# Block kernel, prologue: both low-rank projections tile by tile on the raw input, squares behind them and summed in fours, zero stores moved to after the first group

## Chip, cores, metric

One core of one Trainium2 chip. The time is device time in microseconds of one launch of the whole kernel, median of the runs shown. Everything is float32 in memory; products run on TensorE as three passes over split operands (below).

## The reference, cut to what matters

One layer (`DEPTH` 1) over 512 frames of width 1024. The part that the change touches is the first norm and two narrow column blocks of the input projection, 256 of its 11520 columns: `xw` and `xa` (64 columns each, together "lr0") and `xg` (128 columns, "lr1").

```python
h = rms_norm(x, norm1_g[l])
p = h @ w_in[l]
pa, pb, pg, pc = _split(p, (COLS_A, COLS_B, COLS_GATE, COLS_C))
...
pc = token_shift(pc, rwkv_mu[l])
r, k, v, xw, xa, xg = _split(pc, (D_C, D_C, D_C, R_W, R_A, R_G))
w_log = -jax.nn.softplus(-(rwkv_w0[l] + jnp.tanh(xw) @ rwkv_w2[l])) - 0.5
a = jax.nn.sigmoid(rwkv_a0[l] + xa @ rwkv_a2[l])
g_c = jax.nn.sigmoid(xg) @ rwkv_g2[l]
...
yc = rwkv7_recurrence(rh, decay, kh, vh, kk, ah)
...
m = gate_a * y_a + gate_b * y_b + gate_c * y_c
x = x + m @ w_out[l]
h2 = rms_norm(x, norm2_g[l])
x = x + jnp.square(jax.nn.relu(h2 @ mlp_w1[l])) @ mlp_w2[l]
return rms_norm(x, final_g)
```

The norm's factor is one number per frame, so it can be applied behind a projection of the raw, gain-weighted input instead of in front of it. The kernel does so for four projections: lr0, lr1, and the first blocks of k and r.

## The kernel before, in words

Channels lie on the 128 partitions and frames along the row: `xT` is eight tiles of 128 x 512. A projection of one block of 128 columns is a sum over the eight tiles. Each operand is split into a high part, rounded by a cast on ScalarE, and a low part, the difference formed on VectorE; `mm3` (lines 168 to 171) issues three products per tile, high x high, high x low, low x high, so a projection is 24 matmuls of 128 x 512 into one PSUM buffer.

A framework orders the work. Each instruction has a priority by its place in the program; blocks under `high_priority` are moved ahead by their offset; each engine then works through a fixed list, in order. PSUM pools give three projection buffers (`pp`), two of `pm`, and single ones. Weights come through two raw buffers and three high and low ones (`load_w`, `split_w`).

The prologue (lines 229 to 380):

- POOL clears `zer` and fills `ones`. SP loads the lr0 weight in two halves and `xT` in five pieces, the lr1 weight last. `load_half` (line 151) issues a load and the split of it. ScalarE's own queue loads only the norm's gain `n1t`.
- Two products of `ones` with `zer` (line 258) run before there is data. `warm` loads the Tanh table on ScalarE.
- The loop over the eight tiles forms `xgh` and `xgl`, the split of x times gain, then, at raised priority, the square of the tile on ScalarE; after every second tile VectorE adds the two squares and TensorE sums them over channels with `ones` into `pst` (line 274, four plain float32 products, two passes each). Then the three products of lr0 follow.
- `rsqrt_rows` turns `pst` into `rsb`, the reciprocal root for each frame, in some fifteen short VectorE steps.
- lr1 is projected afterwards as one block (`proj_raw`, line 293), then k0 and r0. `unscaled` multiplies a result with `rsb` into `us`, which empties its PSUM buffer. `pro_scale` makes the normalised rows `hh`, `hl`, tile by tile, which all other projections read.

The main part interleaves two sequences of generators. `krv(g)` makes k, r and v of a group of four heads, `amat(g)` the within-chunk matrices, `inverse` their triangular inverses in two rounds, `chain` runs over the eight chunks. The other sequence, "fill" `fl`, is `ab(q)` for eight blocks, eight projections each, later the gates `gate(q)`. `weave(crit, fill, r)` places r steps of fill behind each step of the critical one; R0 is r beside krv(0). A step of either ends at a `yield`.

The four zero stores (line 874) write a block of zeros from `zer` to `ttd` in device memory, which the chain reads after the inverses have filled the rest. They stand behind krv(0) in the program but wait for nothing except the clearing of `zer`.

At the end, each quarter of the output takes a Sqrt on ScalarE (line 1229). Line 1056 applies a Sqrt to the small tile `epst`, line 1057 fills that tile again.

Of the kernel before, what the change touches and what calls it, by code (L numbers as in the profile page):

```python
# [9 lines left out]
F32 = mybir.dt.float32  # L10
# [19 lines left out]
R0, R1, R2, R3 = 0.85, 0.8, 0.85, 1.6  # L30
NWARM = 2
# [68 lines left out]
def block_kernel(ctx, tc, xt, win, par, mulr, sw, wout, w1, w2, fg, cst, eyes, out):  # L100
# [3 lines left out]
    def tt(o, a, b, op):  # L104
        return v.tensor_tensor(out=o, in0=a, in1=b, op=op)  # L105
# [45 lines left out]
    def load_half(w, src, i):  # L151
        sl = slice(i * S, (i + 1) * S)
        sy.dma_start(w[0][:, sl], src[:, sl])
        split_w(w, sl)
# [88 lines left out]
    wlr = [new_w()]  # L243
    load_half(wlr[0], win[CN[("lr", 0)]], 0)
    for a, n in ((0, 1), (1, 1), (2, 2)):
        sy.dma_start(xT[:, a:a + n], xt[a:a + n].rearrange("k p t -> p k t"))
    load_half(wlr[0], win[CN[("lr", 0)]], 1)
    for a, n in ((4, 2), (6, 2)):
        sy.dma_start(xT[:, a:a + n], xt[a:a + n].rearrange("k p t -> p k t"))
    wlr.append(new_w())  # L250
    for i in range(2):
        load_half(wlr[1], win[CN[("lr", 1)]], i)
# [4 lines left out]
    for i in range(NWARM):  # L257
        pe.matmul(wu, ones, zer, start=True, stop=True)
# [4 lines left out]
    t_lr0 = pp.tile([P, S], F32, tag="pp", name="pp")  # L263
    sqp_ctx = ExitStack()
    sqp = sqp_ctx.enter_context(tc.tile_pool(name="sqp", bufs=1))
    for kt in range(KT):
        sq = (p1 if kt % 2 else sqp).tile([P, S], F32, tag=f"v{kt // 2 % 2}" if kt % 2 else f"sq{kt // 2}", name="sq")
        ac.activation(xgh(kt), xT[:, kt], AF.Copy, scale=n1t[:, kt:kt + 1])
        stt(xgl[:, kt], xT[:, kt], n1t[:, kt:kt + 1], f(xgh(kt)), MUL, SUB)
        with tc.high_priority(offset=OFFP):  # L270
            ac.activation(sq, xT[:, kt], AF.Square)
            if kt % 2 == 1:
                tt(sq, sq, sq_, ADD)
                pe.matmul(pst, ones, sq, start=kt == 1, stop=kt == KT - 1)
        mm3(t_lr0, *wslice(wlr[0], kt), xgh(kt), xgl[:, kt], start=kt == 0, stop=kt == KT - 1)
        sq_ = sq
# [67 lines left out]
    t_lr1 = pp.tile([P, S], F32, tag="pp", name="pp")  # L344
    proj_raw(wlr[1], t_lr1)
# [526 lines left out]

    for g in range(NG):
        gp.dma_start(ttd[32:64, g, :, 0:32], zer[0:32, 0:32].unsqueeze(1).to_broadcast([32, NC * 4, 32]))
# [108 lines left out]
    with tc.tile_pool(name="mw", bufs=2) as mw, \  # L983
# [72 lines left out]
        ac.activation(epst, epst, AF.Sqrt)  # L1056
        gp.memset(epst, EPS)
# [258 lines left out]
```

## Time and profile before

| what | us |
|---|---|
| runs of the kernel | 1028.8 median of 3 (1027.36 to 1030.81) |
| the profiled execution, its own time | 1029.49 |
| its span, first to last instruction | 1027.7 |
| TensorE busy | 1007.2 |
| VectorE busy | 735.1 |
| ScalarE busy | 512.9 |

A line of the profile's timeline gives start, duration, engine, program line, operation, written tile, read tiles and shape; in brackets the idle time of the engine before it and what ended it. PE is TensorE, PEld its weight load, DVE is VectorE, ACT is ScalarE, SPq and POOLq are queues that issue transfers. In a table of stages each engine has its busy time in the stage and its instructions; the last three columns are the granted TensorE clock, the busy share of the DMA engines and GB/s. Matmuls overlap at their ends, so durations of 0.39 us follow each other every 0.23 us.

### The profile page before, as it was taken

Reading aid. Unit: us, or ns where it says so; the run is one execution under the profiler, and the core shown is the slowest. Engines: PE = TensorE matmul, PEld = TensorE weight load, DVE = VectorE, ACT = ScalarE, POOL = GpSimd, SP = SyncE. Lnnn points to the kernel's source line nnn. Section 1 sums busy time; section 2 is a strip of 40 time slices with the busy share of each in tenths; the row PEclk is TensorE's granted clock in tenths of the full one; section 3 lists DMA queues with packets and bytes.
Section 4 is the critical chain, followed back from the end, with each engine's and each line's share of the span. In section 5 each row is a group of like instructions: output and inputs, shape, how many; then the busy total and the mean of one; then the engine's idle time right before and its main releaser. Section 6 shows DMA issues by size and latency. Waiting matters only on the chain. (4 is left out here: it accounts for less than half of the span.)

```text
span 1027.7 us, 15699 instructions
## 1 busy us (share of the span) xinstructions
PE 1007.2 (98%) x6110; PEld 817.7 (80%) x6110; DVE 735.1 (72%) x1251; ACT 512.9 (50%) x757; POOL 110.1 (11%) x179
## 2 busy tenths in 40 slices
PE   8999999999999999999999999999999999999997
PEld 5777877888887788888787877888888888878885
DVE  6997497599865886794668779656554546887775
ACT  7756453655554655456446344435433334454344
POOL 1013011201212112001322100100000000000001
PEclk9999999999999999999999999999999999999999
DMA  6444643734546446434897724544333325644442
GB/s 231 129 123 112 185 134 114 215 107 128 150 134 164 136 126 161 158 95 122 268 256 243 220 87 119 174 132 130 90 99 103 98 87 164 226 127 139 143 166 102
DMA packets 49177, 151.53 MB, mean 147 GB/s; under 512 B 6544, under 2 KB 10128, under 8 KB 48080
## 3 DMA queue, kind: packets, MB, share of 16 engines
q1 hardware_dynamic: 34816, 99.93, 30.6%
q0 software_dynamic: 13568, 49.56, 18.0%
q8 instruction: 48, 0.79, 0.3%
q10 hardware_dynamic: 720, 1.05, 0.3%
q14 instruction: 25, 0.20, 0.1%
HBM read 123.78 MB, written 26.74 MB: 146 GB/s over the span
## 5 line engine op out<-in xcount | busy, mean ns | idle before, releaser
L148 ACT CAST whi<-raw 128x1024 fp32r<-128x1024 f32 (+1 forms) x164 | 169.7, 1037 | 257.0 <-PE pp L170 86.7
L105 DVE TENSOR_TENSOR wlo<-raw,whi 128x1024 fp32r<-128x1024 f32 (+1 forms) x176 | 206.5, 1175 | 91.2 <-ACT whi L148 90.6
L169 PE MATMUL pp<-hh,whi 128*128 128x512 f32 x688 | 271.2, 395 | 0.4 <-DVE rs L108 0.4
L170 PE MATMUL pp<-hl,whi 128*128 128x512 f32 x688 | 270.1, 393 | 0.0
L171 PE MATMUL pp<-hh,wlo 128*128 128x512 f32 x688 | 269.1, 391 | 0.2 <-DVE wlo L105 0.2
L169 PEld LDWEIGHTS pp<-hh,whi 128*128 128x128 f32 x688 | 129.1, 188 | 28.9 <-DVE rs L108 0.9
L171 PEld LDWEIGHTS pp<-hh,wlo 128*128 128x128 f32 x688 | 129.2, 188 | 27.5 <-DVE wlo L105 0.6
L170 PEld LDWEIGHTS pp<-hl,whi 128*128 128x128 f32 x688 | 129.2, 188 | 26.3
L169 PE MATMUL p<-h2h,whi 128*128 128x512 f32 x256 | 100.4, 392 | 0.0
L171 PE MATMUL p<-h2h,wlo 128*128 128x512 f32 x256 | 99.7, 389 | 0.0
L170 PE MATMUL p<-h2l,whi 128*128 128x512 f32 x256 | 99.6, 389 | 0.0
L108 DVE SCALAR_TENSOR_TENSOR r<-p,rsb 128x512 f32<-128x512 f32 x32 | 22.0, 691 | 69.3 <-PE p L171 68.8
L171 PEld LDWEIGHTS p<-h2h,wlo 128*128 128x128 f32 x256 | 48.1, 188 | 10.2
L169 PEld LDWEIGHTS p<-h2h,whi 128*128 128x128 f32 x256 | 48.1, 188 | 9.8
L170 PEld LDWEIGHTS p<-h2l,whi 128*128 128x128 f32 x256 | 48.1, 188 | 9.6
L1225 POOL TENSOR_TENSOR x0f<-xr,fgt 128x512 f32<-128x512 f32 x4 | 5.2, 1296 | 310.6 <-DMA raw<-in_w 301.4
L170 PE MATMUL acc<-ml,whi 128*128 128x512 f32 x64 | 25.0, 391 | 0.0
L171 PE MATMUL acc<-mh,wlo 128*128 128x512 f32 x64 | 25.0, 390 | 0.0
L1076 PE MATMUL acc<-whi,a2h 128*128 128x512 f32 x64 | 24.9, 389 | 0.0
L1076 PE MATMUL acc<-whi,a2l 128*128 128x512 f32 x64 | 24.9, 389 | 0.0
L1076 PE MATMUL acc<-wlo,a2h 128*128 128x512 f32 x64 | 24.9, 389 | 0.0
L1076 PE MATMUL acc<-whi,ah 128*128 128x512 f32 x64 | 24.9, 389 | 0.0
(368 smaller groups left out, 1733.5 us busy)
## 6 DMA issues: line engine op xcount, KB each, us to landing
raw<-in_win SPq DMA_DIRECT2D x88, 512.0 KB, 3.6
raw<-in_w SPq DMA_DIRECT2D x64, 512.0 KB, 3.6
ax<-axd POOLq DMA_DIRECT2D x8, 1024.0 KB, 10.0
axd<-AXt POOLq DMA_DIRECT2D x12, 512.0 KB, 8.7
raw<-in_w SPq DMA_DIRECT2D x24, 256.0 KB, 2.9
bkd<-BKT POOLq DMA_DIRECT2D x4, 1024.0 KB, 15.4
raw<-in_wout SPq DMA_DIRECT2D x8, 512.0 KB, 3.6
bk<-bkd POOLq DMA_DIRECT2D x7, 512.0 KB, 13.0
```

Source lines behind the costliest of these rows:

```text
L105: return v.tensor_tensor(out=o, in0=a, in1=b, op=op)
L108: return v.scalar_tensor_tensor(out=o, in0=a, scalar=s, in1=b, op0=op0, op1=op1)
L148: ac.copy(hi[:, sl], raw[:, sl])
L169: pe.matmul(ps, wh, xh, start=start, stop=False)
L170: pe.matmul(ps, wh, xl, start=False, stop=False)
L171: pe.matmul(ps, wl, xh, start=False, stop=stop)
L1076: pe.matmul(b[i], x_[:, ms], w_, start=id(b[i]) not in begun, stop=last and n == 2, skip_group_check=True)
L1225: gp.tensor_tensor(out=o0, in0=x0, in1=fgt[0], op=MUL)
```

## The change

- Both lr weights are loaded ahead, in halves: the first half of lr1 from ScalarE's queue, the others from SP, between the pieces of x. Their splits stand in the loop, at tiles 0 and 4.
- In the loop each tile has its `xgh` and `xgl`, then the six products of lr0 and lr1, then its square. Squares are added in pairs and the pairs in fours; `pst` has two products instead of four. The raised priority of squares and `pst` goes. lr1 takes a second `pp` buffer from the start; its block behind the loop goes.
- The products before the data are twelve of 128 columns instead of two of 512.
- R0 goes from 0.85 to 1.3.
- The zero stores read a new tile `zz`, from the `vt` buffers, cleared by POOL behind krv(0).
- Lines 1056 and 1057 go.

```diff
-R0, R1, R2, R3 = 0.85, 0.8, 0.85, 1.6
-NWARM = 2
+R0, R1, R2, R3 = 1.3, 0.8, 0.85, 1.6
+NWARM = 12
...
-    wlr = [new_w()]
-    load_half(wlr[0], win[CN[("lr", 0)]], 0)
-    for a, n in ((0, 1), (1, 1), (2, 2)):
+    wlr = [new_w(), new_w()]
+    lr_src = [win[CN[("lr", i)]] for i in range(2)]
+
+    def load_lr(eng, i, h):
+        sl = slice(h * S, (h + 1) * S)
+        eng.dma_start(wlr[i][0][:, sl], lr_src[i][:, sl])
+
+    def load_x(a, n):
         sy.dma_start(xT[:, a:a + n], xt[a:a + n].rearrange("k p t -> p k t"))
-    load_half(wlr[0], win[CN[("lr", 0)]], 1)
-    for a, n in ((4, 2), (6, 2)):
-        sy.dma_start(xT[:, a:a + n], xt[a:a + n].rearrange("k p t -> p k t"))
-    wlr.append(new_w())
-    for i in range(2):
-        load_half(wlr[1], win[CN[("lr", 1)]], i)
+
+    load_lr(sy, 0, 0)
+    load_lr(ac, 1, 0)
+    load_x(0, 1)
+    load_x(1, 1)
+    load_x(2, 2)
+    load_lr(sy, 0, 1)
+    load_lr(sy, 1, 1)
+    load_x(4, 2)
+    load_x(6, 2)
...
     for i in range(NWARM):
-        pe.matmul(wu, ones, zer, start=True, stop=True)
+        pe.matmul(wu[:, 0:P], ones, zer[:, 0:P], start=True, stop=True)
...
-    t_lr0 = pp.tile([P, S], F32, tag="pp", name="pp")
+    t_lr = [pp.tile([P, S], F32, tag="pp", name="pp") for _ in range(2)]
+    t_lr0, t_lr1 = t_lr
...
     for kt in range(KT):
-        sq = (p1 if kt % 2 else sqp).tile(...)
+        if kt % 4 == 0:
+            for w in wlr:
+                split_w(w, slice(kt // 4 * S, kt // 4 * S + S))
         ac.activation(xgh(kt), xT[:, kt], AF.Copy, scale=n1t[:, kt:kt + 1])
         stt(xgl[:, kt], xT[:, kt], n1t[:, kt:kt + 1], f(xgh(kt)), MUL, SUB)
-        with tc.high_priority(offset=OFFP):
-            ac.activation(sq, xT[:, kt], AF.Square)
-            if kt % 2 == 1:
-                tt(sq, sq, sq_, ADD)
-                pe.matmul(pst, ones, sq, start=kt == 1, stop=kt == KT - 1)
-        mm3(t_lr0, *wslice(wlr[0], kt), xgh(kt), xgl[:, kt], start=kt == 0, stop=kt == KT - 1)
+        for w, t in zip(wlr, t_lr):
+            mm3(t, *wslice(w, kt), xgh(kt), xgl[:, kt], start=kt == 0, stop=kt == KT - 1)
+        sq = (p1 if kt % 2 else sqp).tile(...)
+        ac.activation(sq, xT[:, kt], AF.Square)
+        if kt % 2 == 1:
+            tt(sq, sq, sq_, ADD)
+        if kt % 4 == 3:
+            tt(sq, sq, sq4, ADD)
+            pe.matmul(pst, ones, sq, start=kt == 3, stop=kt == KT - 1)
+        if kt % 4 == 1:
+            sq4 = sq
         sq_ = sq
...
-    t_lr1 = pp.tile([P, S], F32, tag="pp", name="pp")
-    proj_raw(wlr[1], t_lr1)
...
     weave(krv(0, GS[0]), fl, R0)
+    zz = p1.tile([P, 2, 2, P], F32, tag="vt", name="zz", bufs=2)[0:32, 0, 0, 0:32]
+    gp.memset(zz, 0.0)
     for g in range(NG):
-        gp.dma_start(ttd[32:64, g, :, 0:32], zer[0:32, 0:32].unsqueeze(1).to_broadcast(...))
+        gp.dma_start(ttd[32:64, g, :, 0:32], zz.unsqueeze(1).to_broadcast(...))
...
-        ac.activation(epst, epst, AF.Sqrt)
-        gp.memset(epst, EPS)
```

More of the change, by code (lines that the diff above doesn't have):

```diff
@@ L266, in block_kernel @@
     for kt in range(KT):
-        sq = (p1 if kt % 2 else sqp).tile([P, S], F32, tag=f"v{kt // 2 % 2}" if kt % 2 else f"sq{kt // 2}", name="sq")
+        if kt % 4 == 0:
+            for w in wlr:
+                split_w(w, slice(kt // 4 * S, kt // 4 * S + S))
         ac.activation(xgh(kt), xT[:, kt], AF.Copy, scale=n1t[:, kt:kt + 1])
         stt(xgl[:, kt], xT[:, kt], n1t[:, kt:kt + 1], f(xgh(kt)), MUL, SUB)
-        with tc.high_priority(offset=OFFP):
-            ac.activation(sq, xT[:, kt], AF.Square)
-            if kt % 2 == 1:
-                tt(sq, sq, sq_, ADD)
-                pe.matmul(pst, ones, sq, start=kt == 1, stop=kt == KT - 1)
-        mm3(t_lr0, *wslice(wlr[0], kt), xgh(kt), xgl[:, kt], start=kt == 0, stop=kt == KT - 1)
+        for w, t in zip(wlr, t_lr):
+            mm3(t, *wslice(w, kt), xgh(kt), xgl[:, kt], start=kt == 0, stop=kt == KT - 1)
+        sq = (p1 if kt % 2 else sqp).tile([P, S], F32, tag=f"v{kt // 2 % 2}" if kt % 2 else f"sq{kt // 2}", name="sq")
+        ac.activation(sq, xT[:, kt], AF.Square)
[6 more added lines that the diff above has]
+            sq4 = sq
         sq_ = sq
@@ L871, in block_kernel @@
     weave(krv(0, GS[0]), fl, R0)
+    zz = p1.tile([P, 2, 2, P], F32, tag="vt", name="zz", bufs=2)[0:32, 0, 0, 0:32]
+    gp.memset(zz, 0.0)
     for g in range(NG):
-        gp.dma_start(ttd[32:64, g, :, 0:32], zer[0:32, 0:32].unsqueeze(1).to_broadcast([32, NC * 4, 32]))
+        gp.dma_start(ttd[32:64, g, :, 0:32], zz.unsqueeze(1).to_broadcast([32, NC * 4, 32]))
     for g in range(NG):
```

## The prediction

> **What bounds the kernel now.** I read the page first, for the shares of the engines, and then a table of stages, because an average over a millisecond says nothing about the stage that is edited.
>
> ```profile
> span 1027.7 us, 15699 instructions
> ...
> PE 1007.2 (98%) x6110; PEld 817.7 (80%) x6110; DVE 735.1 (72%) x1251; ACT 512.9 (50%) x757; POOL 110.1 (11%) x179
> ```
>
> ```profile
> core 0: us, PE busy (x) PEld busy (x) DVE busy (x) ACT busy (x) POOL busy (x), PEclk, DMA share, GB/s
> 0.00:8.26 8.26, 4.18 (x6) 1.47 (x6) 1.43 (x3) 5.57 (x10) 3.93 (x13) 0.98 0.74 230
> 8.26:16.30 8.04, 7.91 (x22) 4.24 (x21) 6.29 (x10) 7.55 (x13) 0.93 (x3) 0.81 1.02 351
> 16.30:40.00 23.70, 23.70 (x103) 18.89 (x102) 23.41 (x52) 15.36 (x24) 0.58 (x1) 1.00 0.45 144
> ...
> 43.70:80.00 36.30, 35.74 (x154) 28.16 (x154) 35.32 (x87) 24.31 (x37) 3.31 (x5) 1.00 0.36 102
> 80.00:100.00 20.00, 18.60 (x134) 14.46 (x133) 15.87 (x24) 11.41 (x19) 5.57 (x10) 1.00 0.44 131
> ...
> 602.00:640.00 38.00, 38.00 (x197) 30.35 (x194) 33.87 (x63) 17.93 (x29) 2.15 (x4) 1.00 0.36 104
> ...
> 1000.00:1028.00 28.00, 20.42 (x91) 16.56 (x89) 14.85 (x25) 13.27 (x29) 5.18 (x4) 0.95 0.30 111
> ```
>
> TensorE is the bound nearly everywhere: outside the first stage its busy time is the stage itself, to a few per cent. So only what moves TensorE's own order is worth anything, and the place where it is not full is the start. The second thing to see is the DVE column from 16.3 to 80 us: 23.41 of 23.70, then 35.32 of 36.30. Over that stretch VectorE is as full as TensorE. A lead that TensorE gains at the start is therefore not automatically kept.
>
> The start in order of time, where the argument lies:
>
> ```profile
> 0.75 0.39 SPq L153 DMA_DIRECT2D raw<-in_win  x1
> ...
> 1.46 3.49 PE L258 MATMUL wu<-zer,ones 128*128 128x512 f32 x4 [1.46 <-POOL one L255]
> ...
> 2.88 1.28 ACT L1056 ACT_TABLE_LOAD   x1
> ...
> 4.29 0.61 ACT L271 ACTIVATE sq<-xT 128x512 f32<-128x512 f32 x1
> ...
> 6.70 0.60 ACT L148 CAST whi<-raw 128x512 fp32r<-128x512 f32 x1
> 6.83 0.69 DVE L105 TENSOR_TENSOR sq<-sq 128x512 f32<-128x512 f32 x1 [6.83 <-ACT sq L271]
> ...
> 7.21 0.72 ACT L268 ACTIVATE xgh<-xT,n1t 128x512 fp32r<-128x512 f32 x1
> ...
> 7.57 1.75 PE L274 MATMUL pst<-sq,ones 128*128 128x512 f32 x2 [2.62 <-DVE sq L105]
> ...
> 8.33 1.42 PE L169 MATMUL pp<-xgh,whi 128*128 128x512 f32 x1
> ...
> 13.17 1.02 PE L274 MATMUL pst<-sq,ones 128*128 128x512 f32 x2
> 13.62 0.80 PE L170 MATMUL pp<-xgl,whi 128*128 128x512 f32 x1
> ...
> 15.80 0.72 DVE L195 STREAM_TRANSPOSE rqw<-pst 128x512 f32<-128x512 f32 x1
> ```
>
> The first product that counts runs at 8.33. ScalarE squares x first (4.29), and TensorE sits idle from 4.95 until the square sum reaches it. The clock view shows what the idle costs:
>
> ```profile
> 10.00:11.00 1.00, 0.88 (x3) 0.28 (x2) 1.00 (x3) 0.67 (x2) 0.00 (x0) 0.50 1.05 404
> ...
> 12.00:13.00 1.00, 0.99 (x4) 0.36 (x3) 0.81 (x2) 1.00 (x3) 0.00 (x0) 1.00 0.99 350
> ```
>
> The granted clock (third column from the end) is 0.50 around 10.5 and 1.00 after 12. The mean of 0.81 over the 8.04 us from 8.26 is 0.19 x 8.04 = 1.5 us of lost clock.
>
> Then TensorE's stream with its marks, the first matmul of the k projection, of the r projection, of the first projection on normalised rows, and where that one runs dry:
>
> ```profile
> 24.39 0.39 PE L169 MATMUL pp<-xgh,whi 128*128 128x512 f32 x1
> ...
> 29.94 0.39 PE L169 MATMUL r<-xgh,whi 128*128 128x512 f32 x1
> ...
> 35.49 0.39 PE L169 MATMUL pp<-hh,whi 128*128 128x512 f32 x1
> ...
> 39.14 0.39 PE L171 MATMUL pp<-hh,wlo 128*128 128x512 f32 x1
> ...
> 40.09 0.66 PE L169 MATMUL pp<-hh,whi 128*128 128x512 f32 x2
> ```
>
> One projection of 24 matmuls is 35.49 - 29.94 = 5.55 us, 0.231 each. And VectorE, which makes the normalised rows:
>
> ```profile
> 23.02 0.71 DVE L202 STREAM_TRANSPOSE rsb<-rqq 128x512 f32<-128x512 f32 x1
> 23.66 1.18 DVE L105 TENSOR_TENSOR wlo<-raw,whi 128x1024 fp32r<-128x1024 f32 x1
> ...
> 27.75 0.74 DVE L108 SCALAR_TENSOR_TENSOR hl<-xT,n1t,hh 128x512 fp32r<-128x512 f32 x1
> ...
> 39.50 0.69 DVE L105 TENSOR_TENSOR us<-pp,rsb 128x512 f32<-128x512 f32 x1
> ...
> 42.97 0.74 DVE L108 SCALAR_TENSOR_TENSOR hl<-xT,n1t,hh 128x512 fp32r<-128x512 f32 x1
> ```
>
> TensorE meets VectorE here with almost no slack: the tiles of `hl` come from 27.75 to 43.6, and the second PSUM buffer of `pp` is free only when `us` at 39.50 has emptied the lr1 result; TensorE starts its second normalised projection at 40.09.
>
> **The change part by part.** *The squares.* Summing in fours takes two of the four `pst` matmuls away. One is two passes; from 13.17 the next matmul, which needs 0.39 by itself, ends at 14.42 and so began its own work near 14.03: 0.86 us each, 1.7 us of TensorE saved. VectorE gets two additions more, at the 0.69 of the 6.83 row, 0.60 where they follow each other: +1.2 us.
>
> *The order.* The splits of both lr weights, `xgh`, `xgl` and the six products of a tile come before its square. The first tile needs the first weight half, the first x tile, two splits and `xgh`. In the trace the first half is issued at 0.75 and ScalarE can read x0 at 4.29. The second half-weight now goes out beside it on ScalarE's queue, 256 KB, which at the 371 to 404 GB/s of the busy rows is 0.7 us more in front of or between the bytes of x0. Two casts at 0.53 pace and one scaled copy at 0.71 from about 4.2 to 4.5 put the first product at 5.8 to 6.2; I take 6.0, 2.3 us earlier than 8.33. From there a tile is six products, 1.39 us on TensorE, against about 1.2 to 1.3 on ScalarE (`xgh` 0.71, square 0.61, both overlapping a little) and 1.1 on VectorE, so TensorE sets the pace except at the second weight halves, two casts of 0.6, for which I allow 0.7 in all. Sum: 6.0 + 48 x 0.231 + 1.7 + 0.7 = 19.5 for both projections, against 24.39: **4.9 us of lead**.
>
> *The bytes.* The zero stores go out between 1.88 and 9.5 on POOL's queue, beside x:
>
> ```profile
> 4.00:5.00 1.00, 0.95 (x2) 0.00 (x0) 0.00 (x0) 0.89 (x3) 0.47 (x1) 1.00 0.78 154
> ...
> 6.00:7.00 1.00, 0.00 (x0) 0.00 (x0) 0.17 (x1) 0.83 (x2) 0.00 (x0) 1.00 1.04 387
> ```
>
> ```profile
> xT<-in_xt SPq DMA_DIRECT2D x1, 512.0 KB, 8.7
> ...
> L874 POOL DMA_DIRECT2D ttd<-zer x4: 784/795/981, 1.9 to 8.7; - x4
> ```
>
> In their slice the engines move 154 GB/s where they move 387 two slices later. Two such slices lose about 0.4 MB, 1.1 us; that pays for most of the 512 KB of lr1, 1.4 us, which now stands ahead of x4 to x7. So the last x tiles land about when they do now (issued near 3.6, 8.7 us to land: 12.3), between 10.8 and 12.6. They are wanted at 13, so this is hidden; were they 2 us later still, TensorE would wait that long.
>
> The Trainium skill, "DMA: Bandwidth & Descriptors", rules for kernel authors, says that issuing from several engines gives no bandwidth, since all run on the same 16 DMA engines. By that rule ScalarE's queue brings nothing sooner and 1.4 us of lr1 bytes count in full; no row here has two hardware queues loading at once, so nothing here confirms it.
>
> *The warm-up.* 12 products of 128 columns instead of 2 of 512: at the 3.49 us for 1024 columns of the 1.46 row, 1536 columns are 5.2 us at the low clock, until 6.7; if the clock rises at about 4.6 the last ones run twice as fast and end near 5.6. Between 0 and 0.7 us in front of the first product; I take 0. What it buys is that TensorE no longer idles before the work: up to the 1.5 us of lost clock, already in the 4.9, whose sum is at full clock.
>
> The Trainium skill, "TensorE: Matmul & The Clock Gate", Part 1, puts the rise behind one busy window of about 3.4 us that runs free of the kernel, and the fall behind an idle one. The trace agrees: busy 3.49 us, idle 2.62, then 0.50 for about three slices. By that rule the phase of the window alone could move the gain by up to 1.5 us between runs.
>
> *The removed square root* on `epst`. It was placed at 2.88, not at the end; its table load of 1.28 is on ScalarE before x has landed, worth nothing there. The reload that it forces later also goes:
>
> ```profile
> 23.35 1.28 ACT L391 ACT_TABLE_LOAD   x1
> ```
>
> That one stands before a weight cast and the shift of lr: 0.3 us at most on the path. The four zero stores reappear after krv(0), at 0.8 us of POOL each and behind the release of a `vt` buffer. The row behind them:
>
> ```profile
> 98.12 1.60 POOL L539 DMA_DIRECT2D lad<-AXt  x2 [11.15 <-DVE AXt L105]
> ```
>
> POOL sits idle for 11.15 us before it, waiting for VectorE; 3.3 us of issue fit in. Uncovered, they would delay those stores by 3.3 us, which only the inverse behind later groups reads. Cost 0.
>
> *The weave, R0 0.85 to 1.3.* krv(0) has 20 steps: 17 fill steps become 26. A fill chain of 8 projections has 32 steps, so a step is 8 x 5.55 / 32 = 1.4 us and 9 steps move 12.5 us of TensorE's work from later to here. It changes no total. It helps where VectorE is full, because fill asks less of VectorE per microsecond; it costs later cover, and the row of 602 to 640 is full, with gates behind the chain of chunks, 35 us of it, against 12.5 taken. I take 0, between -1.4 (the idle of 80 to 100) and +2.
>
> *What comes late next.* TensorE, 4.9 us ahead, reaches the normalised rows at 30.6. VectorE has by the stage table 1.43 + 6.29 + 23.41 + 3.6 = 34.7 us of work up to the last `hl`, in 36.8 us from its first instruction at 6.83. It now starts near 4.2, with 1.2 more to do: 2.6 - 1.2 = 1.4 us of lead if it idles as much as now, 3.5 if it never idles, none if the square sum, now last, holds it up. I take 2.0. The second `pp` buffer then comes free at 38.1 instead of 40.1, with one tile (0.69) more of the first projection behind TensorE: 2.7 us of lead there, and 0.3 from the table load and the gap at 39.14, 3.0; half of the 0.56 us that 43.7 to 80 has of idle is put to the extra fill, 0.2 to 0.3. So TensorE gives 1.7 of its 4.9 back and **3.2 us remain**. The tail is not touched.
>
> The profiled execution took 1029.49, its span and 1.8 us around it, 0.07% above the median 1028.8. Its span should become 1027.7 - 3.2 = 1024.5; the median 1028.8 - 3.2 = **1025.6**.
>
> **The rivals.** *VectorE takes nearly all back.* It is at 99% from 16.3 to 40; if its lead is below 1, TensorE waits for `hl` and the buffer, and only about 1 us is left: 1027.8. For it: the DVE column. Against: weight splits that now sit behind 23.02 can be done before.
>
> *The whole lead is kept.* With the splits of 1.18 out of the way and more fill beside krv(0), TensorE never waits: 4.9 and a little of the idle later, 5.3: 1023.5. For it: 40 to 100 has 2 us of idle to recover. Against: one free `pp` buffer until `us`.
>
> *Slower: the root is late.* The last square sum is now behind all six products of the last tile, near 18.9 instead of 15.8. If the small steps of the root are threaded between long additions as now (15.80 to 23.73, 7.9 us), `rsb` comes at 26.9 instead of 23.73, 3.2 later, and every `hh` and `hl` with it. With the 1.2 of extra additions, less the 0.69 and 0.3 above, the loss is 3.4: 1032.2. It decides, beyond what can be told from no change, from an `rsb` at about 26.6 on. Against: the `xgl` and lr splits that VectorE threads in there now are done earlier.
>
> **How the numbers follow.** The measurement tells about 0.3% from no change, 3.1 us, so 1025.7 and 1031.9 are the limits. The first case, part of the lead kept, has 0.40 and its own range 1024.2 to 1027.0; as it lies on the limit, half of it counts on either side. Nearly all taken back 0.24, all kept 0.24, root late 0.12. Faster 0.20 + 0.24 = 0.44, same 0.20 + 0.24 = 0.44, slower 0.12. TensorE's idle time between start and tail, 1027.7 - 1007.2 less 4.1 before 8.26 and 7.6 in the last 28 us, is 8.8 us; a shifted order deals these waits anew, for which I allow 1.7 us below the whole lead and 2.4 above the case that loses it: 1021.8 to 1030.2.
>
> **What would show it.** First product of `pp` at about 6 and granted clock 1.00 from there; four `pst` passes, not eight; the lr products done at 19 to 20; no table load before Exp; `rsb` at 23 to 26; the first matmul on `hh` near 30, and gaps of some 2 us on TensorE between 30 and 40, put down to `hl` or `us`. Wrong would be: a first product later than 7.5, `rsb` after 27, new gaps in 80 to 110 or in the chain of chunks around 500 to 600.

## The result, and the profile after

The change makes the kernel slower: median 1036.84 us (1035.27 to 1038.19, 6 runs) against 1029.62 us (1027.36 to 1030.81, 6 runs) on the same chip, ratio 1.0071, 95% interval 1.0055 to 1.0088. That is 7.2 us more. The forecast was 1025.6 us with a range up to 1030.2; the time lies outside, on the other side. (Every ratio here is against runs of the kernel before on the same chip.) The profiled execution took 1038.19 us, its span is 1036.4.

The page of the changed kernel, busy time by engine:

```profile
span 1036.4 us, 15737 instructions
...
PE 1010.6 (98%) x6126; PEld 822.0 (79%) x6126; DVE 737.6 (71%) x1253; ACT 510.6 (49%) x754; POOL 109.6 (11%) x179
```

TensorE's work grew by 3.4 us (1010.6 against 1007.2), part of which is time at a lower clock. Its idle time grew from 20.5 to 25.8 us. The stages of the changed kernel, with the columns of the table of before (length; busy time of PE, PEld, DVE, ACT, POOL; granted clock; DMA share; GB/s):

```profile
0.00:8.26 8.26, 6.80 (x29) 6.38 (x30) 2.52 (x4) 4.96 (x8) 1.51 (x10) 1.00 0.73 249
8.26:16.30 8.04, 8.04 (x35) 5.99 (x33) 7.66 (x13) 8.01 (x16) 0.00 (x0) 1.00 0.77 270
16.30:40.00 23.70, 21.47 (x83) 15.34 (x82) 22.25 (x55) 13.17 (x20) 0.82 (x2) 0.97 0.53 162
31.00:45.00 14.00, 11.77 (x40) 7.86 (x39) 13.04 (x21) 8.64 (x15) 0.70 (x1) 0.88 0.34 114
```

The last stretch in the kernel before:

```profile
31.00:45.00 14.00, 14.00 (x62) 11.01 (x61) 13.89 (x22) 8.98 (x15) 0.58 (x1) 1.00 0.39 123
```

Up to 31 us the change does what it says: the clock is 1.00 from the first stage (0.81 in the second stage before), and the stage from 8.26 to 16.30 holds 35 matmuls instead of 22. Then TensorE does 40 matmuls from 31 to 45 us where it did 62. Its instructions and VectorE's there, in order of time:

```profile
6.70 1.15 PE L169 MATMUL pp<-xgh,whi 128*128 128x512 f32 x2
...
19.32 1.02 PE L290 MATMUL pst<-sq,ones 128*128 128x512 f32 x2
...
24.12 0.71 DVE L202 STREAM_TRANSPOSE rsb<-rqq 128x512 f32<-128x512 f32 x1
...
25.57 1.23 DVE L105 TENSOR_TENSOR wlo<-raw,whi 128x1024 fp32r<-128x1024 f32 x1 [0.74 <-ACT whi L148]
...
29.71 0.74 DVE L108 SCALAR_TENSOR_TENSOR hl<-xT,n1t,hh 128x512 fp32r<-128x512 f32 x1
...
36.28 0.50 PE L170 MATMUL pp<-hl,whi 128*128 128x512 f32 x1 [1.18 <-DVE hl L108]
...
40.34 0.69 DVE L105 TENSOR_TENSOR us<-pp,rsb 128x512 f32<-128x512 f32 x1
...
44.67 0.74 DVE L108 SCALAR_TENSOR_TENSOR hl<-xT,n1t,hh 128x512 fp32r<-128x512 f32 x1
```

The last sum of squares runs at 19.32 (14.74 before), the root `rsb` is there at 24.12 (23.02), the first `hl` at 29.71 (27.75), `us` at 40.34 (39.50), the last `hl` at 44.67 (42.97). Every one of these rows, all of which TensorE needs, is later, though TensorE is earlier.

To see where time is lost over the whole kernel I worked out a **lag** from the trace. Each matmul counts with the usual distance between the ends of two matmuls of its kind in the profile of before (warm-up and `pst` count nothing). For an instant of the profile of before, the lag is how much later the other kernel has done the same amount of TensorE work; below zero it is ahead. "Again" is a second profile of the same kernel.

| lag in us at | 35 | 45 | 70 | 100 | 250 | 420 | 500 | 540 | 690 | end |
|---|---|---|---|---|---|---|---|---|---|---|
| before again | +1.9 | +1.9 | +1.9 | +1.9 | +1.9 | +2.0 | +2.0 | +5.8 | +5.5 | +6.1 |
| after | -4.1 | +0.9 | +2.6 | -0.6 | +1.2 | +2.5 | +2.5 | +4.0 | +5.6 | +8.8 |
| after again | -3.9 | +0.9 | +2.6 | -0.5 | +1.2 | +2.3 | +2.3 | +6.0 | +7.5 | +9.1 |

So a lead of 4 us is there at 35 us and gone at 45, and some 8 us are lost from 100 us to the end. The second profiles show what belongs to the order of the instructions: up to 500 us the two profiles of after agree within 0.2 us, and the two of before keep one distance, given at the start. The distance of the two of before is in the main that of the clock: granted 0.81 on average from 8.26 to 16.30 us in the first and 0.58 in the second, which over the first 22 us is 1.7 and 3.4 us of work not done. At the start of the chain of chunks (500 to 540 us) executions of one kernel differ by up to 4 us, so of the 8 us that the first two profiles put behind 100 us a part is chance: the second profile of before falls back by 4.2 us there itself. Waits of TensorE in the changed kernel (total, times, longest):

```profile
PE pp L169 <- DVE ks L108: 1.9, 1, 1.9
...
PE pA L544 <- DVE AXt L105: 1.7, 2, 1.3
...
PE tp L958 <- ACT sj L964: 1.5, 1, 1.5
...
PE pp L170 <- DVE hl L108: 1.5, 2, 1.2
PE acc L1091 <- DVE wlo L105: 1.2, 1, 1.2
```

They are small and lie all over the kernel: 60 to 65 us (`ks`), about 400 us (`AXt`), 31 to 45 us (`hl`), about 696 us (`sj`) and 902 us (`wlo`).

### The profile page after: what moved, and what is told of

It is laid out like the page before. It is cut to its first block, busy times and chain, and to the rows that moved or that the text cites. A ratio compares the mean times of both kernels' runs of the same rounds, so it can differ in the third digit from the quotient of the medians.

```text
span 1036.4 us, 15737 instructions
## 1 busy us (share of the span) xinstructions
PE 1010.6 (98%) x6126; PEld 822.0 (79%) x6126; DVE 737.6 (71%) x1253; ACT 510.6 (49%) x754; POOL 109.6 (11%) x179
## 4 chain that ended last, share of the span: by engine, by line
PE 64%; DVE 7%; DMA 5%; issue 2%; ACT 2%; POOL 0%; DVEq 0%; POOLq 0%; ACTq 0%
PE acc L1091 11%; PE pp L169 9%; PE pp L170 9%; PE pp L171 9%; PE p L171 5%; PE p L170 5%; PE p L169 5%; DMA raw<-in_w 2%; DMA rt<-rtd 2%; DVE wlo L105 2%; PE py L680 1%; PE acc L169 1%; PE acc L171 1%; PE acc L170 1%; DVE ym L105 1%
## 5 line engine op out<-in xcount | busy, mean ns | idle before, releaser
L1091 PE MATMUL acc<-wlo,ah 128*128 128x512 f32 x64 | 25.0, 391 | 1.2 <-DVE wlo L105 1.2
L169 PE MATMUL acc<-mh,whi 128*128 128x512 f32 x64 | 24.6, 392 | 0.4 <-ACT mh L749 0.4
```

The costliest lines, as they stand in the source:

```text
L169: pe.matmul(ps, wh, xh, start=start, stop=False)
L1091: pe.matmul(b[i], x_[:, ms], w_, start=id(b[i]) not in begun, stop=last and n == 2, skip_group_check=True)
```

## The experiments

Theories: **A**, the lead is lost between 31 and 45 us since the normalised rows come no earlier; **B**, R0 at 1.3 costs later; **C**, any edit deals the planner's order anew, so that the sum of small waits is chance. A fourth, **D**, came with R0: its cost is that the fill stands some ten steps further on at every later stage (nine, 26 instead of 17; the expectations say ten).

### R0 back to 0.85 on the changed kernel

```
-R0, R1, R2, R3 = 1.3, 0.8, 0.85, 1.6
+R0, R1, R2, R3 = 0.85, 0.8, 0.85, 1.6
```

> The changed kernel with the weave beside krv(0) put back to 0.85. Theory A (TensorE's lead of 4 us at 31 us is lost between 31 and 45 us, because the normalised rows come 2 us later and the granted clock falls; the weave adds little): the loss between 31 and 45 us stays, some 5 us, and the time lies at 1033 to 1037. Theory B (the weave at 1.3 is the cause, by the order that it deals for everything behind): back to 1026 to 1030. Theory C (any edit deals the order anew, and the sum of later waits scatters by 2 to 4 us): the stage up to 45 us as in the changed kernel, the rest anywhere within 4 us.

Measured 1034.5 us against 1029.86, ratio 1.0041 (1.0016 to 1.0066). R0 costs about 3 us on the new prologue; the rest of the loss stays. Lag: -4.2 at 35 us, -0.1 at 45, +4.1 at 70, then +3.9 from 100 to 500 us and +4.1 at the end. So with R0 at 0.85 the order behind 100 us keeps pace with before; for this kernel that speaks against theory C. Windows 31 to 45 and 58 to 80 us of this kernel, and its longest wait with what ScalarE did ahead of it:

```profile
31.00:45.00 14.00, 11.59 (x45) 7.40 (x44) 13.73 (x22) 9.30 (x15) 0.70 (x1) 1.00 0.32 104
58.00:80.00 22.00, 18.28 (x72) 14.32 (x71) 20.33 (x39) 13.16 (x19) 2.62 (x5) 0.92 0.36 102
```

```profile
59.10 1.99 ACT L148 CAST whi<-raw 128x1024 fp32r<-128x1024 f32 x2 [3.86 <-PE pp L170]
...
63.37 0.50 PE L169 MATMUL pp<-hh,whi 128*128 128x512 f32 x1 [3.17 <-ACT g L783]
```

Two casts of weights, held up by TensorE, stand in ScalarE's order ahead of the copies that empty the `pp` buffers, and TensorE then waits 3.17 us for a buffer. This second hole I had not seen in advance.

### R0 at 1.3 alone, on the kernel before

```
-R0, R1, R2, R3 = 0.85, 0.8, 0.85, 1.6
+R0, R1, R2, R3 = 1.3, 0.8, 0.85, 1.6
```

> The kernel before with only the weave beside krv(0) at 1.3. Theory A: the start is that of before, no loss at 31 to 45 us, time within 2 us of before, 1028 to 1032. Theory B: 1035 to 1038. Theory C: 1026 to 1034, with the difference in waits scattered behind 100 us.

Measured 1035.2 us against 1029.86, ratio 1.0044 (1.0017 to 1.0070): 4.5 us by the ratio, so B holds for this edit by itself. Lag +1.8 at 70 us (from the start of this execution), -1.5 at 100, +1.0 at 250, +3.6 at 420. From 395 to 430 us, first the kernel before, then this one:

```profile
395.00:430.00 35.00, 35.00 (x156) 28.92 (x155) 24.75 (x45) 21.03 (x30) 5.66 (x9) 1.00 0.71 204
```

```profile
395.00:430.00 35.00, 33.53 (x192) 27.69 (x191) 19.90 (x28) 15.06 (x20) 6.45 (x9) 0.95 0.60 164
```

### The new prologue alone

The changed prologue, with R0 0.85, the zero stores at the start and the square root on `epst` as before.

```
-R0, R1, R2, R3 = 1.3, 0.8, 0.85, 1.6
+R0, R1, R2, R3 = 0.85, 0.8, 0.85, 1.6
...
-    zz = p1.tile([P, 2, 2, P], F32, tag="vt", name="zz", bufs=2)[0:32, 0, 0, 0:32]
-    gp.memset(zz, 0.0)
     for g in range(NG):
-        gp.dma_start(ttd[32:64, g, :, 0:32], zz.unsqueeze(1).to_broadcast([32, NC * 4, 32]))
+        gp.dma_start(ttd[32:64, g, :, 0:32], zer[0:32, 0:32].unsqueeze(1).to_broadcast([32, NC * 4, 32]))
...
+        ac.activation(epst, epst, AF.Sqrt)
+        gp.memset(epst, EPS)
```

> The new prologue alone (loads, loop, squares in fours, twelve short warm-up products) with the weave at 0.85, the zero stores and the Sqrt on epst as before. Theory A: lead of about 4 us at 31 us, lag of about 1 us at 45 us, time 1030 to 1036. Theory B: 1025 to 1029. If the zero stores in the early stage cost what I gave them, the first x tiles land about 1 us later than in the changed kernel.

Measured 1036.84 us, ratio 1.0060 (1.0037 to 1.0083). The prologue by itself costs 6 us. With the zero stores beside them the large x loads land in 8.7 us (median) instead of 7.4. `rsb` comes at 27.17 here, 2.9 us later than with the zero stores moved, but the last `pst` only 0.6 us later (19.92 against 19.35): the rest is order, as two long weight splits stand among the short steps of the root here, one of them after a wait of 1.06 us for its cast. The lag is +1.4 at 45 us and +6.6 at 70.

### Squares at raised priority in the changed kernel

```
+        with tc.high_priority(offset=OFFP):
             ac.activation(sq, xT[:, kt], AF.Square)
             if kt % 2 == 1:
                 tt(sq, sq, sq_, ADD)
             ...
```

> The changed kernel with the squares, their sums and the two pst products at raised priority again, as before the change. Theory A with the late root as its reason: rsb comes 2 to 4 us earlier than 24.1, the first hl with it, the gap of TensorE at 31 to 41 us shrinks from some 4 us to under 2 and the granted clock stays at 1.00; time 1031 to 1034. If it is the weight splits that hold hl back and not the root: hl comes at 29.7 whatever rsb does, and the time stays near 1037.

Measured 1039.55 us, ratio 1.0077 (1.0050 to 1.0105). The last `pst` goes from 19.32 to 16.99, but `rsb` comes at 23.84, only 0.3 us earlier, as VectorE has the splits and sums of the tiles to do between. So neither account of the expectation came: the root was not earlier by 2 to 4 us, and the first `hl` came at 29.17, 0.5 earlier. The last `hl` came 2.2 us earlier, at 42.43, as VectorE waited less on the way (below). Lag -1.2 at 45 us instead of +0.9; but of these 2.1 us 0.6 are left at 70 us and 0.3 at 250. In the profile 5.3 us of wait for `ax` follow at the start of the chain, the place where executions differ by 4 us anyway. The median of ten executions is no better than that of the changed kernel: 2 us won at 45 us were not kept, and that speaks for theory C or for a second bound behind 45 us.

### A raw xb projection in the hole

The first recurrent input projection (`xb` of row 0) is made on the raw rows behind `r0`, in a spare PSUM bank, and scaled by `rsb` where its result was copied; R0 0.85. The three raw projections of k, r and xb are raised by 30, which lets the last `pst` slip to 21.42; `rsb` moves to a pool that lives longer.

```
-    rsb = pro.tile([P, S], F32, name="rsb")
+    rsb = p1.tile([P, S], F32, name="rsb")
...
+    t_xb0 = pc.tile([P, S], F32, tag="py", name="xb0")
+    with tc.high_priority(offset=30):
+        for n, t in ((("k", 0), t_k0), (("r", 0), t_r0), (("xb", 0), t_xb0)):
+            proj_raw(load_w(win[CN[n]]), t)
...
+        if q == 0:
+            for _ in range(3):
+                yield
+            tt(px, t_xb0, rsb, MUL)
```

> The changed kernel with R0 at 0.85 as before, and the first recurrent input projection (xb of row 0) made on the raw rows as well, right behind r0, into a spare PSUM bank; its row is scaled by rsb where it was copied. Its 24 products (5.5 us) need none of the normalised rows. Theory A (TensorE starves at 31 to 45 us since the normalised rows come at VectorE's pace whatever TensorE's lead): TensorE is busy 13.3 us or more of the 14 us from 31 to 45 (11.6 with R0 0.85 without this edit), and the lead of 4 us over the kernel before still stands at 45 us; if nothing is lost at 60 to 70 us either, the time is 1026 to 1027. Rival (VectorE as a whole is the bound up to about 70 us, so TensorE's lead can't be kept by any order): the lead stands at 45 us but is gone by 70 to 80 us, lag there +2 to +4 as without the edit, 1032 to 1034.

Measured 1031.27 us against 1030.83, ratio 0.9999 (0.9980 to 1.0019): the loss of 1.0041 is gone. The same windows as above:

```profile
31.00:45.00 14.00, 12.43 (x53) 9.49 (x53) 13.86 (x22) 9.88 (x16) 0.00 (x0) 1.00 0.21 75
58.00:80.00 22.00, 20.16 (x86) 16.00 (x86) 21.11 (x44) 13.57 (x20) 2.85 (x5) 1.00 0.48 138
```

TensorE does 53 matmuls in the hole (45 without) and 86 instead of 72 in the next stage; the lag is -2.6 at 45 us and -0.8 at 70. The rival, VectorE as a whole as the bound up to 70 us, had the lag at +2 to +4 there, and that did not come: VectorE's rows are even later here (`rsb` 28.30, last `hl` 45.68), and TensorE is ahead all the same. But the lead is not kept either: of 4.2 us at 35 us 0.8 are left at 70 and none at 190 (+0.2). The 13.3 us that I expected in the hole were not reached, and the 1026 to 1027 us that I expected neither: the edit wins back what the prologue lost, and no more.

### Giving the fill steps back

Three kernels with R0 1.3 take the fill steps out again, as ten (one or two more than R0 brings forward): from group 1 alone, from group 1 with the raw xb projection, from group 2 with it.

```
-FILL = {1: (4, 13, 5), 2: (36, 13, 5), 3: (4, 13, 5)}
+FILL = {1: (0, 9, 3), 2: (36, 13, 5), 3: (4, 13, 5)}
```

```
+FILL = {1: (4, 13, 5), 2: (26, 13, 5), 3: (4, 13, 5)}
```

> The changed kernel with R0 at 1.3, but the ten fill steps that R0 brings forward are taken out again right behind group 0 (FILL of group 1 from 4, 13, 5 to 0, 9, 3), so that from about 190 us on every stage meets the same fill work as in the kernel before. Theory D (late shift): what the changed kernel loses behind 390 us (TensorE busy 33.5 of 35 us at 395 to 430 and 46.6 of 50 us at 495 to 545, against 35.0 and 48.1 before) comes from the fill work being ten steps further on at those places; here both windows are back at 34.8 or more and 47.8 or more, the lag behind the kernel before stays at 0 to +2 us from 100 us to the end, and the time is 1030 to 1032 with the kernel before at 1029.9. Theory C (any edit deals the order anew): the lag grows somewhere else behind 100 us, 1033 to 1038. A third way: group 1 misses the fill that was taken from it, the lag jumps by 2 us or more at 120 to 180 us.

> Both edits together on the changed kernel: R0 1.3 with the ten fill steps taken out of group 1, and the raw xb projection of row 0. Theories A and D together: the lead of 4 us stands at 45 us, 1 to 2 us of it go at 60 to 70 us, nothing goes behind 390 us: 1026 to 1028, faster than the kernel before. Rival (VectorE is the bound up to 70 us): lag 0 to +2 at 80 us, 1030 to 1032. Theory C: a loss of 2 us or more at a place where none of the other kernels has one, 1032 to 1038.

> As the kernel with R0 1.3 and the raw xb projection of row 0, but the ten fill steps are taken out of group 2 (lead of 36 to 26) and not of group 1. Theory A: lag -4 at 40 us, -3 at 60 us, -1.5 to -3 at 100 to 300 us, as there. What follows at 500 us tells two accounts of the 2.4 us lost there apart: if the weights' transfers and the chain's first loads collide wherever the fill stands (raw and ax issued within 3 us of each other), 2 us or more are lost again and the time is 1030 to 1034; if that was the accident of one order (the cast of a weight that lands late stands ahead of the chain's copy on ScalarE), the lag stays below 0 and the time is 1026 to 1029.

Measured: 1035.89 us (ratio 1.0036, 1.0020 to 1.0052), 1034.61 us (1.0030, 1.0013 to 1.0046) and 1035.7 us against 1031.18 (1.0041, 1.0022 to 1.0060). One half of the expectation came: TensorE is busy 35.00, 35.00 and 34.98 us from 395 to 430 us. The other half did not. The first two lose 3.9 and 2.5 us at the start of the chain, the third 6.4 us between 250 and 300 us (one profile each). The times expected with the steps back, 1030 to 1032, 1026 to 1028 and 1026 to 1029 or 1030 to 1034 us, were missed, and what theory C had forecast for the first two came: 1033 to 1038 and 1032 to 1038 us. The start of the chain in the second, ScalarE and TensorE:

```profile
498.40 1.05 ACT L148 CAST whi<-raw 128x1024 fp32r<-128x1024 f32 x1 [6.53 <-DMA raw<-in_win]
499.46 1.28 ACT L846 ACT_TABLE_LOAD   x1
500.76 0.69 ACT L846 ACTIVATE g<-pp,part 128x512 f32<-128x512 f32 x1
501.47 0.58 ACT L676 COPY u<-pu 64x512 f32<-64x512 f32 x1
```

```profile
502.10 1.15 PE L692 MATMUL pu<-u,tc 64*64 64x64 f32 x32 [2.94 <-ACT u L676]
```

A weight that lands late (its load goes out at 488.62 beside the chain's own loads) holds up ScalarE, and the chain's copy stands behind its cast. So the pair 1.0030 with R0 1.3 and 0.9999 with 0.85 is a third price, 3.1 us, of R0 with its steps given back, paid at another place than in the changed kernel. Theory D, that the cost is the shift of the fill, holds for 395 to 430 us and not for the sum.

### The zero stores alone, twice

```
+    zz = p1.tile([P, 2, 2, P], F32, tag="vt", name="zz", bufs=2)[0:32, 0, 0, 0:32]
+    gp.memset(zz, 0.0)
     for g in range(NG):
-        gp.dma_start(ttd[32:64, g, :, 0:32], zer[0:32, 0:32].unsqueeze(1).to_broadcast([32, NC * 4, 32]))
+        gp.dma_start(ttd[32:64, g, :, 0:32], zz.unsqueeze(1).to_broadcast([32, NC * 4, 32]))
```

> The kernel before with the stores of zeros alone moved behind group 0's stage, from a buffer of their own. If the stores cost nothing where they stand now: lag 0 up to 85 us and within 1 us to the end, 1029 to 1031. Theory C: the planner deals later parts anew and the lag moves by 2 us or more somewhere behind 85 us, 1027 to 1036.

> The kernel before with only the zero stores moved, once more. Account: the four stores of 128 KB went out at 1.9 to 9 us beside the first x tiles; without them the five x loads land earlier (the two large ones in about 6.0 us instead of 7.9) and the first sum of squares comes about 1 us sooner, which every later instruction keeps: 1.5 to 3 us faster, ratio 0.9970 to 0.9985. If the gain before was chance: ratio 0.9990 to 1.0010, and the first sum of squares at 7.5 us in some profile.

Measured 1029.79 us, ratio 0.9978 (0.9964 to 0.9993), and 1029.3 us, ratio 0.9987 (0.9972 to 1.0002): about 1.3 to 2.3 us faster, by the second interval not told apart from no change. The gain is small, but no version is faster. Transfers from 0 to 30 us (count, size, median us to landing), in the kernel before and with the stores moved:

```profile
xT<-in_xt SPq DMA_DIRECT2D x3, 512.0 KB, 7.9
...
ttd<-zer POOLq DMA_DIRECT2D x4, 128.0 KB, 6.7
```

```profile
xT<-in_xt SPq DMA_DIRECT2D x3, 512.0 KB, 6.0
```

```profile
6.45 1.12 PE L274 MATMUL pst<-sq,ones 128*128 128x512 f32 x2 [1.21 <-DVE sq L105]
```

The first sum of squares runs at 6.45 instead of 7.57 (6.53 in the second run). The Trainium skill, "DMA: Bandwidth & Descriptors", Queues, rings and completion order, says that each DMA engine goes round between the queues that have work, a packet at a time. The rows agree as far as they go: beside four stores on POOL's queue, first read at about 491 us, the x loads on SP's queue took 1.9 us longer, 1.4 by the second run (6.5); that it goes by packets no row shows.

A rival for the gain is the clock. In these two profiles it is 1.00 all through the first 22 us, where those of the old prologue with the stores at the start lost 1.7 us once and 3.4 twice; the lead of these two over the first profile of before is 1.6 and 0.7 us. That the shorter wait of the first sum (1.2 us instead of 2.6) is what kept the clock up was not tested.

### Zero stores moved and the narrow warm-up, on the kernel before

```
-NWARM = 2
+NWARM = 12
...
-    pe.matmul(wu, ones, zer, start=True, stop=True)
+    pe.matmul(wu[:, 0:P], ones, zer[:, 0:P], start=True, stop=True)
```

> The kernel before with the two parts of the change that touch neither the order of the projections nor the fill: zero stores moved, and twelve narrow warm-up products in place of two wide ones. Theory A: a lead in the prologue is kept if the normalised rows come earlier with it; the sums of squares here run ahead as in the kernel before, so 1 to 1.5 us of TensorE's low clock in the first 8 us are gained and kept: lag -1 to -3 from 20 us to the end, 1026 to 1028.5. Theory C: the warm-up moves the order in the prologue and some of the gain is lost again by 70 us: 1029 to 1031.

Measured 1029.54 us, ratio 0.9987 (0.9969 to 1.0005). Not better than the zero stores alone: `rsb` is at 23.80, and the lag +0.8 from 20 us on. The expected 1026 to 1028.5 us did not come. Here the clock fell, to 0.50 from 12 to 15 us, although the stores are moved and the warm-up is narrow; that is 1.7 us.

### Both kernels once more

> The changed kernel once more, for a second profile of it. Loss by loss this tells what belongs to the order of the instructions from what differs from one execution to the next: waits that are fixed by the order should come again at the same place within 0.5 us (normalised rows at 31 to 45 us, pA for AXt at about 400 us, the start of the chain at 520 to 540 us); waits that a transfer sets (rt, ax, the weights at about 902 us) may differ by a microsecond or two. If all of the lag behind 390 us is of the second kind, a time of 1032 or less would be among the changed kernel's executions; with the order as its cause it stays at 1034 to 1039.

> The kernel before once more, for a second profile. Its first 20 us in the profile at hand have a wait of 2.6 us of the sums of squares for VectorE, and with only the zero stores moved it was 1.2 us, in the same order of instructions: if that is chance between executions, the second profile of before shows another value than 2.6 us and its lag at 20 us is anywhere from -1.6 to +0.5; if the zero stores had cost it, the wait is 2.6 us again. Time 1027 to 1031.

1038.52 and 1035.67 us; their lags are in the first table. From 495 to 545 us TensorE is busy 48.05 us in the first profile of before and 44.55 in the second; 46.65 and 44.52 in those of after:

```profile
495.00:545.00 50.00, 48.05 (x665) 38.73 (x665) 29.15 (x48) 24.04 (x35) 10.69 (x20) 1.00 1.02 284
```

```profile
495.00:545.00 50.00, 44.55 (x577) 35.72 (x577) 27.83 (x46) 19.94 (x29) 11.74 (x21) 1.00 1.01 270
```

So this part of the difference between my first two profiles is not the change. The windows 31 to 45 us (11.99 against 11.77) and 395 to 430 us (33.53 against 33.51) came again. In the second profile of before the first `pst` waited 2.2 us: with the zero stores there 2.6, 2.3 and 2.2 us in three profiles, without them 1.2 and 1.3.

### A third raw buffer for weights in the prologue

```
-    wlr = [new_w(), new_w()]
+    wlr = [new_w()]
+    wlr.append((pro.tile([P, D], F32, name="raw1"), ...))
```

> The changed kernel with R0 0.85 and a third buffer for raw weights in the prologue (the second low-rank weight has its own), so that the loads of the next weights needn't wait for the splits. If the late load is what makes the rows late: no wait of ScalarE for a weight at 24 us, the first hl at 27.5 to 28.5 us instead of 29.4, TensorE busy 12.8 or more of the 14 us from 31 to 45 (11.6 without), 1 to 2.5 us less than the 1034.5 without the buffer: 1032 to 1033.5. Rival (the amount of VectorE's work sets it): the wait is gone but the first hl and the gaps of TensorE stay within 0.5 us, 1034 to 1035.

> The same third buffer together with the raw xb projection of row 0, R0 0.85. If the late weights cost the 1.6 us that TensorE lost at 31 to 45 us with the raw xb projection alone (busy 12.4 of 14), the lead is 4 us at 45 us, and 1 to 2 us more than there are left at the end: 1029 to 1030.5 with the kernel before at 1031. Rival: within 0.5 us of the kernel without the buffer, 1031 to 1031.5.

Both have R0 0.85, the second also the raw xb projection. Measured 1038.82 us (ratio 1.0074, 1.0049 to 1.0100) and 1034.48 us (1.0022, 1.0000 to 1.0045): both read worse than without the buffer (1.0041 and 0.9999), though the intervals overlap. The test did not isolate what it was made for. The free buffer lets the load of k's weight stand ahead of the last x tiles on SP's queue; they are issued at 9.43 instead of 3.69, TensorE waits for `xgh`, the clock falls, and `rsb` comes at 28.15 and 29.83. First kernel:

```profile
8.45 1.65 PE L169 MATMUL pp<-xgh,whi 128*128 128x512 f32 x3 [2.42 <-ACT xgh L283]
...
9.05 0.33 SPq L137 DMA_DIRECT2D raw<-in_win  x1
9.43 0.95 SPq L254 DMA_DIRECT2D xT<-in_xt  x2
```

So no run takes the 0.74 us that VectorE waits for a weight at 25.57 in the changed kernel out by itself. But as unplanned shifts of the rows these runs help with the next question.

## Why the prediction was wrong

**The lead in the prologue: right.** First product at 6.70 (forecast 6.0), granted clock 1.00 from there, 4.9 us of lead forecast and a lag of -5.1 at 20 us measured. The closeness is partly luck: the 1.5 us of lost clock in that sum belong to the profile that was read, and against the second profile of before the lead is 7.0. The prediction's remark that the phase could move the gain by about 1.5 us between runs came true (1.7 us lost in one profile of before and 3.4 in the other). Its "the trace agrees" goes too far for the fall: the waits before it, 2.62 and 2.22 us, are shorter than the idle window that it names.

**What comes late next: the step that failed first.** It took the last `hl` 2.0 us earlier, out of a sum of VectorE's start, work and idle time, and kept 3.2 us for TensorE. The same sum from the traces, from VectorE's first instruction to the start of the last `hl` (work is VectorE's busy time between the two):

| kernel | start | work | idle | last `hl` |
|---|---|---|---|---|
| before | 6.83 | 34.10 | 2.04 | 42.97 |
| after | 4.17 | 36.39 | 4.11 | 44.67 |
| after again | 4.14 | 36.46 | 4.09 | 44.69 |
| after, squares first | 4.02 | 35.95 | 2.47 | 42.43 |

The start was right (2.66 us earlier, 2.6 forecast). The added work is 2.3 us and not 1.2, as short steps on `spt`, 1.05 us of them, moved ahead of the last `hl` beside the two additions. The idle time was to shrink by 0.6 and grew by 2.1: in the changed kernel 2.4 us of it are for the weight casts `whi` of ScalarE (0.8 before). So the last `hl` is 1.7 us late instead of 2.0 early.

The rival "the root is late" named the direction, but its mechanism is not what the trace shows. VectorE does not wait for the last `pst`, which ends at 20.34; it is at a weight split then, behind a wait for a cast, and takes the first step of the root, `rqw`, after that:

```profile
19.88 1.22 DVE L105 TENSOR_TENSOR wlo<-raw,whi 128x1024 fp32r<-128x1024 f32 x1 [0.43 <-ACT whi L148]
...
21.03 0.71 DVE L195 STREAM_TRANSPOSE rqw<-pst 128x512 f32<-128x512 f32 x1
```

With the squares first, `pst` was 2.3 us earlier and `rsb` 0.3. And its threshold was wrong: it was reckoned by the end of `rsb`, at 26.6, and the lead is gone with `rsb` ending at 24.83 (start 24.12). From the profiles:

| kernel | last `pst` | `rsb` | last `hl` | lag at 35 | lag at 45 |
|---|---|---|---|---|---|
| before | 14.74 | 23.02 | 42.97 | 0 | 0 |
| before again | 16.61 | 24.89 | 44.85 | +1.9 | +1.9 |
| before, R0 1.3 | 16.52 | 24.81 | 44.76 | +1.8 | +1.8 |
| before, zero stores late | 13.15 | 21.43 | 41.38 | -1.6 | -1.6 |
| the same again | 13.98 | 22.28 | 42.23 | -0.8 | -0.7 |
| after | 19.32 | 24.12 | 44.67 | -4.1 | +0.9 |
| after, R0 0.85 | 19.35 | 24.30 | 43.48 | -4.2 | -0.1 |
| prologue alone | 19.92 | 27.17 | 45.01 | -3.6 | +1.4 |
| after, squares first | 16.99 | 23.84 | 42.43 | -3.3 | -1.2 |
| after, raw3, R0 0.85 | 22.47 | 28.15 | 45.99 | -1.5 | +2.4 |
| after, raw xb, R0 0.85 | 21.42 | 28.30 | 45.68 | -4.2 | -2.6 |

With the old prologue the last `hl` starts 19.95 us behind `rsb` in all five rows, and TensorE's lag is the lateness of `rsb`, to 0.1 us; but that is one fixed order shifted as a whole from the first 20 us on, and does not tell the root from anything else there. With the new prologue the distance is not fixed (17.4 to 20.6 us), and the lag at 45 us is the lateness of the last `hl` less 0.6 to 0.8 us (44.67 - 42.97 = 1.7 against 0.9; 45.99 - 42.97 = 3.0 against 2.4), whether TensorE was 4.2 or 1.5 ahead at 35. Only the raw xb projection breaks the link: `hl` 2.7 us late, lag -2.6, because 24 products that need no `hl` lie in the hole. So TensorE is held by the rows that VectorE makes, and a lead in front of them is worth nothing unless they come earlier. Of their 1.7 us of lateness 1.1 stood at `rsb` and a further 0.6 came between `rsb` and the last `hl`, where VectorE was idle for 1.70 us instead of 0.26. Instead of 3.2 us kept, 0.9 were lost. That the rows hold TensorE is shown by the raw xb projection; what makes the rows late is read from the traces, as no run takes the waits for the casts out alone.

**The clock fell in the hole.** That was not in the sum; it costs 1.7 us (0.88 on average over the 14 us). Between 38 and 42 us of the changed kernel matmuls run at half the clock (columns: length, TensorE's busy time, granted clock, DMA share, GB/s):

```profile
38.00:39.00 1.00, 0.74 (x2) 0.68 0.40 160
39.00:40.00 1.00, 1.00 (x3) 0.50 0.00 0
40.00:41.00 1.00, 1.00 (x3) 0.50 0.00 0
```

**The weave at 0: wrong, and by its middle values outside its bounds of -1.4 to +2.** R0 costs 4.5 us on the kernel before (1.8 to 7.2), about 3.0 on the new prologue (1.0071 against 1.0041) and 3.1 beside the raw xb projection with the fill steps given back (1.0030 against 0.9999), the last two as differences of ratios whose intervals are some 2 us to either side. With the new prologue it fills the second hole, at 60 to 70 us: lag -0.6 at 100 us, +3.8 without. Then it gives back more than it won: +2.5 at 420 us and, in the two profiles, 4.8 and 3.1 us more from 540 us to the end, where the kernel with R0 0.85 loses 0.4. My only bound on the cost was cover at the end of the chain; the first loss, 1.5 us at 395 to 430 us, was none of that but another piece of fill beside the same critical work. Which waits behind 540 us R0 brings by itself was not settled.

**The zero stores at 0: wrong in sign.** I saw that they halve the bytes of a slice (154 GB/s) and counted it only as room for the second weight. Alone they are worth 1.3 to 2.3 us by the medians, by earlier loads of x, by a clock that did not fall, or by both.

**The order dealt anew.** I allowed 1.7 to 2.4 us for it. With R0 at 0.85 the lag grows by 0.3 us from 100 us to the end (1.3 with the prologue alone). With R0 at 1.3 it cannot be told how much is R0's shift and how much the order dealt anew, beside up to 4 us of chance at the start of the chain: the three kernels that give the steps back each lose 2.5 to 6.4 us at a place of their own, so theory C is not excluded there.

As a sum by ratios: the prologue alone +6.2 us, moving the zero stores and dropping the square root -2.0 (1.0060 to 1.0041), R0 +3.1, together 7.3; measured 7.2. The sum closes by construction, as each term is the step to the next ratio, so it confirms nothing; the single terms are uncertain by 2 to 3 us each, and the square root was not tested alone.

## What to carry to other kernels

Behind a reduction over all input (here the root of the norm), follow the engine that makes the rows from its start to the last row that is needed, with its work and its waits: a lead on another engine was worth nothing until work independent of these rows was put into the hole, and moving the reduction itself 2.3 us forward moved the root by 0.3. Look for what the engine waits for, here the casts of another engine that stand in a fixed order. Stores that nobody reads soon are better kept out of the first microseconds, though here the gain is at the edge of what was measured. Before a difference between two profiles is explained, take a second profile of each: here 4 us at one place and 1.9 us in the prologue were chance, while the rest came again within 0.2 us.

## What the runs showed of the hardware

Two profiles of one kernel follow each other within 0.2 us over 450 us, from 45 to 500 us, with thousands of instructions on five engines; nearly all the spread comes in at two places, 1.9 us in the first 20 us of the kernel before and 2 to 4 us at the start of the chain, where TensorE waits for the load of `ax` for 0.7 us in one profile of after and for 2.7 in the other. The first of them is the clock, and it comes in steps. Summed over the first 22 us, one minus the granted clock is 1.7 us in the first profile of before, 3.4 in the second and in that of R0 at 1.3 alone, 0 in both with the zero stores moved, 1.7 with the narrow warm-up beside that, and 1.7 and 3.4 in the two with a third raw buffer. Each of these six that fell lost 1.7 us or twice that, at half clock, and for the kernel before it was the one in one profile and the other in the next.

The clock can fall without a long idle stretch: in the changed kernel the longest wait ahead of the 0.50 above was 1.18 us, with TensorE busy 0.10, 0.72, 0.70 and 0.74 in the four slices from 35 to 39 us, and nearly the same in its second profile. With the fill taken out of group 1 the slices are 0.10, 0.72, 0.71 and 0.74, and the clock stayed at 1.00. The Trainium skill, "TensorE: Matmul & The Clock Gate", A second HAM failure mode: psum-queue depth-cycling, describes such a fall from frequent short idling; the first of these kernels agrees, and the second shows that the same pattern can pass.
